# First weights in a free slot, later adaLN pieces, and the norm weight folded into the first tokens of a gated short-convolution layer

## The chip, the core and the metric

The kernel runs on one core of a Trainium2 chip. The metric is the device time of one execution in microseconds. TensorE (PE) does the matrix products, VectorE (DVE) and ScalarE (ACT) the elementwise work, GpSimd (POOL) a few set-up operations, and SyncE (SP) issues nearly all DMA transfers. Each engine works through its own queue in the order in which the program was written down for it, and waits there for semaphores.

## The reference, cut to what matters

One layer is computed in f32, with 256 tokens, D = 2048, E = 4096:

```python
h = rmsnorm(x, norm_g)                       # (256, 2048)
shift, scale, gate = split(silu(c) @ ada_w + ada_b, 3)
h = h * (1.0 + scale) + shift
b_gate, c_gate, v, g = split(h @ w_in, 4)    # w_in (2048, 4 * 4096)
y = b_gate * causal_conv3(c_gate * v, conv_w) * silu(g)
x = x + gate * (y @ w_out)                   # w_out (4096, 2048)
out = rmsnorm(x, final_g)
```

All weights are read once from HBM. f32 products are made of three products of split operands: each weight tile and each activation tile is split into `hi` (rounded to the matmul's format) and `lo` (the remainder), and `hi*hi + hi*lo + lo*hi` is summed.

## The kernel before

**Features.** D is cut into 16 rows of 128, called k. The tokens are scaled by `rstd`, turned by TensorE and kept in `xs[0..3]` (four k in each). When shift and scale of a k are known, `features(k)` writes `hT[:, k]`: ScalarE the rounded half (`hh_`, 128x256), VectorE first the full value back into `xs` and then the remainder (`hl_`).

**adaLN.** Shift and scale come from `ada_w` (2048 rows), for two k at a time: group 0 gives k = 0 and 1, group 1 gives k = 2 and 3, and so on to group 7. Group 0 is loaded whole at the start (`at0`) and summed by VectorE into `gv0`, with three of its 16 rows on TensorE. TensorE then sums over the partitions with `ones` (`sum0(None, ...)`). Every later group is cut into 8 *pieces* of 0.5 MB, each two DMAs and two VectorE operations `gv += at * silu_c`. When a group's last piece is summed, TensorE turns `gv` (`tp_g`, L459, four transposes), ScalarE sums each (L461), VectorE makes shift and scale, and `features` follows for its two k.

**Products of the first half (chunks 0 to 3).** A chunk is 512 columns of one of the four quarters of `w_in`. `plan()` writes out a list of *steps*. A step is one chunk or two, one quarter q, and a stretch of k; per chunk and k there are 12 *products* (L471: 128x128 weights on 128x256 tokens). Steps are numbered from 0 here. Each step takes one *load* of 1 MB per two k (load n belongs to step n up to step 13; load 1 has 0.5 MB), which ScalarE casts into `hi` (*cast n*, L338) and VectorE turns into `lo` (*remainder n*, L339). Loads have three buffers, and so have `hi` and `lo`. Step 0 uses `raw0` (0.5 MB), which takes one of the three load buffers. At a step's end ScalarE copies each chunk's sum from PSUM to SBUF (L503) if it is the chunk's first; a later step of the same chunk either *seeds* PSUM with the kept sum ahead of its products and copies it back behind them (ScalarE, L519 and L503), or adds the kept sum at the end (VectorE, L505). `plan()` decides this by its own estimates of the engines' load.

adaLN pieces are dealt out between loads: every load adds `SHARE` = 1.5 to a `credit`, and each whole unit of it issues one piece. `plan()` also estimates when a group's features are ready, and lets a step's stretch of k reach only that far.

**Around it.** `idle(n, ...)` puts `IDLE[n]` products of ones on TensorE, whose results nobody reads. `pinned` keeps each engine's opening instructions in the order of the code, up to the features of k = 0 and 1; behind that a scheduler places the instructions. After the first half comes the second half of the columns (`mm_b`, from 382 us) and the output products (`mm_o`, from 731 us).

Of the kernel before, what the change touches and what calls it, by code (L numbers as in the profile page):

```python
# [17 lines left out]
KT = D // P  # L18
# [6 lines left out]
CT = 4  # L25
# [29 lines left out]
def plan():  # L55
# [2 lines left out]
    pieces = [(sum(ADA[:g]), nk, i) for g, nk in enumerate(ADA) if g for i in range(4 * nk)]  # L58
    load, pe, dve, act = 0.0, 4.0, 0.0, 0.0
    burst = SLOT // P  # L60
    credit = 0.0

    def ada():
        nonlocal load, dve
# [27 lines left out]
    while new or any(k < KT for k in done.values()):  # L92
        before = []
        hi = sum(r <= pe for r in ready)
        if new:
            p = new.pop(0)
# [32 lines left out]
def short_conv_layer(ctx: ExitStack, tc: tile.TileContext, x, c, norm_g, ada_w, ada_b, w_in, conv_w, w_out, final_g, out):  # L129
    nc = tc.nc  # L130
# [16 lines left out]
    def slot(shape, name, dtype=F32):  # L147
        return slots.tile(shape, dtype, tag="slot", name=name)

    def raw_tile(name):  # L150
        return wpool.tile([P, SLOT], F32, tag="raw", name=name, bufs=3)
# [44 lines left out]
    rows2 = const.tile([96, P], F32, tag="rows2", name="rows2")  # L196
    HX = D // 2
    GIVE = 300
    IDLE = (20, 8, 22, 4, 4, 5, 7, 6)
    xt = [[slot([P, HX], f"x{t}{dh}") for dh in range(2)] for t in range(TT)]  # L200
    for t in range(TT):
        for dh in range(2):
# [8 lines left out]
    for n in range(KT // 4):  # L211
# [5 lines left out]
            for s in range(2):  # L217
                nc.sync.dma_start(at[:, j : j + kk, s, :], adas[:, 4 * n + j : 4 * n + j + kk, s, 0 : NK0 * P])
        first_ada.extend(at[:, i] for i in range(4))
    raw0 = raw_tile("raw0")  # L220
    for k in range(NK0):
        first_load(raw0, k)

# [37 lines left out]
    tp_v = turn(rows1, 0, 64, None)  # L261
    gT = vec[:, 0:16]
    b_shift = vec[:, 16:32]
    b_scale1 = const.tile([P, KT], F32, tag="bsc", name="b_scale1")
    idle(1, turned[2])
    tp_c = turn(rows2, 0, 96, None)
    idle(2, turned[2])
# [43 lines left out]
    def modulate(k0, nk, sums):  # L311

        ks = slice(k0, k0 + nk)
        if nk == 1:
            nc.vector.tensor_scalar(
                out=scale[:, ks], in0=sums[1], scalar1=b_scale1[:, ks], scalar2=gT[:, ks], op0=ALU.add, op1=ALU.mult
            )
            nc.scalar.activation(shift[:, ks], sums[0], AF.Identity, bias=b_shift[:, ks])
        else:
            nc.vector.tensor_tensor(out=scale[:, ks], in0=sums[1], in1=b_scale1[:, ks], op=ALU.add)  # L320
            nc.vector.tensor_tensor(out=scale[:, ks], in0=scale[:, ks], in1=gT[:, ks], op=ALU.mult)
            nc.vector.tensor_tensor(out=shift[:, ks], in0=sums[0], in1=b_shift[:, ks], op=ALU.add)
        for k in range(k0, k0 + nk):
            features(k)

    def features(k):
        hf = xs[k // CT][:, k % CT, :]
        nc.scalar.activation(hh_[:, k], hf, AF.Identity, bias=shift[:, k : k + 1], scale=scale[:, k : k + 1])
        nc.vector.tensor_scalar(
            out=hf, in0=hf, scalar1=scale[:, k : k + 1], scalar2=shift[:, k : k + 1], op0=ALU.mult, op1=ALU.add  # L330
        )
        nc.vector.tensor_tensor(out=hl_[:, k], in0=hf, in1=hh_[:, k].bitcast(F32), op=ALU.subtract)

    def split(raw, n, lo_tag="lo"):
# [25 lines left out]
    for k in range(KT):  # L360
# [2 lines left out]
            nc.vector.tensor_scalar_mul(gv0, first_ada[k], c_k)  # L363
        elif k not in ON_PE:
            nc.vector.scalar_tensor_tensor(out=gv0, in0=first_ada[k], scalar=c_k, in1=gv0, op0=ALU.mult, op1=ALU.add)
    nc.vector.tensor_scalar_add(b_scale1, vec[:, 32:48], 1.0)

    scaled_x(0)
    scaled_x(1)
# [11 lines left out]
    idle(4, turned[3])  # L381
    turn_x(turned[3], 3)
    nc.scalar.copy(xs[3], turned[3])
    tp_idle = psum.tile([P, CT, T], F32, tag="mm", name="tp_idle")
    sum0_of(1)
    idle(5, tp_idle)
# [6 lines left out]
    lo0 = wpool.tile([P, SLOT], F32R, tag="lo", name="lo", bufs=3)  # L393
    w = CT * P
    for k in range(NK0):
        nc.vector.tensor_scalar(
            out=scale[:, k : k + 1], in0=sums0[k][:, 1:2], scalar1=b_scale1[:, k : k + 1], scalar2=gT[:, k : k + 1],
            op0=ALU.add, op1=ALU.mult,
        )
    for k in range(NK0):  # L400
        c = slice(k * w, (k + 1) * w)
        nc.scalar.copy(hi0[:, c], raw0[:, c])
        nc.scalar.activation(shift[:, k : k + 1], sums0[k][:, 0:1], AF.Identity, bias=b_shift[:, k : k + 1])
        nc.vector.tensor_tensor(out=lo0[:, c], in0=raw0[:, c], in1=hi0[:, c].bitcast(F32), op=ALU.subtract)
        features(k)
    pinned.close()
    pieces0 = [(hi0, lo0)]

# [376 lines left out]
```

## Time and profile before

| | |
|---|---|
| median of 3 runs | 915.22 us (914.12 to 916.56) |
| profiled execution | 914.62 us, of which the span from first to last instruction 912.8 us |
| mean granted TensorE clock | 0.996 |
| TensorE busy | 897.6 us, 98% of the span |
| VectorE, ScalarE busy | 628.8 us (69%), 452.3 us (50%) |
| HBM read | 224.49 MB, 248 GB/s over the span |
| first product (L471) | 26.97 us |

Rows of a timeline begin with start and duration in us; a bracket at the end tells how long the engine idled before the row and what ended that. Operands are written output<-input by the tiles' names. A count xN merges equal instructions that follow each other; matmul durations overlap, so starts are to be subtracted, not durations added. A chain is followed back from the last instruction, at each step to what released it; releasers are inferred from semaphore events, and where a wait is for several things it is put down to the one that ended last.

### The profile page before, as it was taken

What the parts mean: (1) busy time and instruction counts of PE and PEld (TensorE: products, weight loads), DVE (VectorE), ACT (ScalarE), POOL (GpSimd) and SP (SyncE); (2) the same over time, 40 slices, a digit from 0 to 9 for tenths busy, and PEclk for the clock granted to TensorE, in tenths of its full rate; (3) what the DMA queues carried; (4) which work ended last, traced back from release to release, by engine and by line L of the source; (5) the groups of instructions that cost most, each with busy time, mean ns of one, the idle gap of its engine ahead of it and who ended that gap; (6) DMA issues with size and microseconds to landing.
All of it is one profiled execution on the core that took longest, in us unless ns stands there. A gap on an engine that the chain in (4) does not pass through costs nothing.

```text
span 912.8 us, 16305 instructions
## 1 busy us (share of the span) xinstructions
PE 897.6 (98%) x7091; PEld 865.4 (95%) x7091; DVE 628.8 (69%) x603; ACT 452.3 (50%) x431; POOL 2.3 (0%) x9
## 2 busy tenths in 40 slices
PE   7899999999999999999999999999999999999996
PEld 7899999999999999999999999999999988888885
DVE  5888989899988998995555455545455544555882
ACT  6678876544545755554333443334433333443333
POOL 1000000000000000000000000000000000000000
PEclk9999999999999999999999999999999999999999
DMA  9999999999898778876655666656656486665542
GB/s 307 377 379 358 339 353 340 353 343 345 295 352 284 254 250 279 284 235 210 201 190 186 191 200 204 190 185 193 199 193 198 142 333 224 201 201 193 185 139 92
DMA packets 146775, 227.64 MB, mean 249 GB/s; under 512 B 5456, under 2 KB 103808, under 8 KB 146320
## 3 DMA queue, kind: packets, MB, share of 16 engines
q1 hardware_dynamic: 146576, 226.51, 73.8%
q8 instruction: 55, 0.90, 0.4%
q14 instruction: 16, 0.13, 0.0%
q0 software_dynamic: 96, 0.08, 0.0%
q10 hardware_dynamic: 32, 0.01, 0.0%
HBM read 224.49 MB, written 2.10 MB: 248 GB/s over the span
## 4 chain that ended last, share of the span: by engine, by line
PE 94%; DMA 3%; ACT 2%; issue 0%; ACTq 0%; SPq 0%; DVE 0%
PE mm_b L471 38%; PE mm_s L471 36%; PE mm_o L681 6%; PE mm_o L682 6%; PE mm_o L683 6%; DMA at<-in_ada_w_dram 3%; ACT hi L338 1%; DMA x<-in_x_dram 1%; ACT mm_s L519 0%; ACT acc L503 0%; PE tp_g L459 0%; PE ps_gate L620 0%; ACT tp_g L461 0%; ACT big L695 0%; ACT big L692 0%
## 5 line engine op out<-in xcount | busy, mean ns | idle before, releaser
L471 PE MATMUL mm_b<-hT,hi 128*128 128x256 f32 x2048 | 348.4, 276 | 0.0
L471 PE MATMUL mm_s<-hT,hi 128*128 128x256 f32 x2048 | 336.6, 277 | 1.5 <-ACT hi L338 1.2
L471 PEld LDWEIGHTS mm_b<-hT,hi 128*128 128x128 f32 x2048 | 308.3, 188 | 0.0
L471 PEld LDWEIGHTS mm_s<-hT,hi 128*128 128x128 f32 x2048 | 299.5, 188 | 2.0 <-ACT hi L338 1.4
L471 PE MATMUL mm_b<-hT,lo 128*128 128x256 f32 x1024 | 282.6, 276 | 0.0
L471 PE MATMUL mm_s<-hT,lo 128*128 128x256 f32 x1024 | 262.2, 277 | 0.0
L339 DVE TENSOR_TENSOR lo<-raw,hi 128x2048 fp32r<-128x2048 f32 x64 | 146.7, 2292 | 130.1 <-ACT hi L338 130.1
L338 ACT CAST hi<-raw 128x2048 fp32r<-128x2048 f32 x64 | 122.5, 1913 | 197.6 <-PE mm_b L471 150.5
L471 PEld LDWEIGHTS mm_b<-hT,lo 128*128 128x128 f32 x1024 | 192.2, 188 | 0.1
L471 PEld LDWEIGHTS mm_s<-hT,lo 128*128 128x128 f32 x1024 | 183.1, 188 | 0.0
L338 ACT CAST hi<-raw_s 128x2048 fp32r<-128x2048 f32 (+1 forms) x64 | 121.7, 1901 | 93.2 <-PE mm_s L471 78.6
L339 DVE TENSOR_TENSOR lo<-raw_s,hi 128x2048 fp32r<-128x2048 f32 (+1 forms) x64 | 145.4, 2271 | 23.9 <-ACT hi L338 23.4
L339 DVE TENSOR_TENSOR lo<-raw_o,hi 128x2048 fp32r<-128x2048 f32 x32 | 73.3, 2290 | 65.2 <-ACT hi L338 65.2
L338 ACT CAST hi<-raw_o 128x2048 fp32r<-128x2048 f32 x32 | 61.0, 1907 | 106.8 <-PE mm_o L683 84.0
L682 PE MATMUL mm_o<-lo,y 128*128 128x512 f32 x256 | 99.3, 389 | 0.0
L683 PE MATMUL mm_o<-hi,y 128*128 128x512 f32 x256 | 99.3, 389 | 0.0
L681 PE MATMUL mm_o<-hi,y 128*128 128x512 f32 x256 | 99.3, 389 | 0.0
L452 DVE SCALAR_TENSOR_TENSOR gv<-at,silu_c,gv 128x512 f32<-128x512 f32 x105 | 78.5, 749 | 2.5 <-DMA at<-in_ada_w_dram 0.9
L683 PEld LDWEIGHTS mm_o<-hi,y 128*128 128x128 f32 x256 | 48.0, 188 | 10.0
L681 PEld LDWEIGHTS mm_o<-hi,y 128*128 128x128 f32 x256 | 48.1, 188 | 10.0
L682 PEld LDWEIGHTS mm_o<-lo,y 128*128 128x128 f32 x256 | 48.0, 188 | 9.9
L503 ACT COPY acc<-mm_s 128x1024 f32<-128x1024 f32 x43 | 43.6, 1018 | 27.9 <-PE mm_s L471 27.8
(107 smaller groups left out, 385.8 us busy)
## 6 DMA issues: line engine op xcount, KB each, us to landing
raw<-in_sc_w_in_dram SPq DMA_DIRECT2D x64, 1024.0 KB, 5.7
raw_s<-in_sc_w_in_dram SPq DMA_DIRECT2D x63, 1024.0 KB, 7.2
raw_o<-in_sc_w_out_dram SPq DMA_DIRECT2D x32, 1024.0 KB, 5.2
at<-in_ada_w_dram SPq DMA_DIRECT2D x126, 256.0 KB, 7.3
at_g<-in_ada_w_dram SPq DMA_DIRECT2D x32, 512.0 KB, 6.6
x<-in_x_dram SPq DMA_DIRECT2D x4, 512.0 KB, 6.6
big<-in_x_dram SPq DMA_DIRECT2D x2, 1024.0 KB, 8.6
out_dram<-big SPq DMA_DIRECT2D x4, 512.0 KB, 2.9
```

The lines of the kernel that those rows point to most:

```text
L338: nc.scalar.copy(hi[:, :n], raw[:, :n])
L339: nc.vector.tensor_tensor(out=lo[:, :n], in0=raw[:, :n], in1=hi[:, :n].bitcast(F32), op=ALU.subtract)
L452: nc.vector.scalar_tensor_tensor(out=gv, in0=at4[:, i], scalar=c_k, in1=gv, op0=ALU.mult, op1=ALU.add)
L471: mm = last_mm[0] = nc.tensor.matmul(dst, w, h[:, k], start=begins and left, stop=ends, skip_group_check=True)
L503: nc.scalar.copy(acc[ch, q], bank)
L681: nc.tensor.matmul(po, yh, hi[:, o], start=opens, stop=False, skip_group_check=True)
L682: nc.tensor.matmul(po, yh, lo[:, o], start=False, stop=False, skip_group_check=True)
L683: nc.tensor.matmul(po, yl, hi[:, o], start=False, stop=ct == NCT - 1, skip_group_check=True)
```

## The change

Four edits. `raw0` is taken from the pool of general slots instead of from the three load buffers. `credit` starts at -1.5, so each piece is issued one load later; since `plan()` also moves its estimates, the list of steps changes. The norm weight is multiplied into `xs[0]` for k = 0 and 1 by ScalarE as soon as that tile is there, so that shift and scale of these k are made by one VectorE operation per k (`sh_sc`), ScalarE's separate `shift` going away. And idle products are moved: `IDLE` 22 to 20 ahead of the transposes, 7 to 11 ahead of group 0's last sums, 6 to 4 behind them; their number stays 76.

```diff
-    credit = 0.0
+    credit = -1.5
...
-    IDLE = (20, 8, 22, 4, 4, 5, 7, 6)
+    IDLE = (20, 8, 20, 4, 4, 5, 11, 4)
...
-    raw0 = raw_tile("raw0")
+    raw0 = slot([P, NK0 * CT * P], "raw0")
...
-    b_scale1 = const.tile([P, KT], F32, tag="bsc", name="b_scale1")
+    b_scale1 = vec[:, 32:48]
+    b_both = vec[:, 16:48].rearrange("p (s k) -> p s k", s=2)
+    sh_sc = const.tile([P, KT // 2, 2], F32, tag="shsc", name="sh_sc")
...
-            features(k)
+            features(k, scale[:, k : k + 1], shift[:, k : k + 1])
...
-    def features(k):
+    def features(k, sc, sh):
...
     nc.scalar.copy(xs[3], turned[3])
+    for k in range(NK0):
+        nc.scalar.activation(xs[0][:, k, :], xs[0][:, k, :], AF.Copy, scale=gT[:, k : k + 1])
...
     for k in range(NK0):
-        nc.vector.tensor_scalar(
-            out=scale[:, k : k + 1], in0=sums0[k][:, 1:2], scalar1=b_scale1[:, k : k + 1], scalar2=gT[:, k : k + 1],
-            op0=ALU.add, op1=ALU.mult,
-        )
+        nc.vector.tensor_tensor(out=sh_sc[:, k], in0=sums0[k][:, 0:2], in1=b_both[:, :, k], op=ALU.add)
     for k in range(NK0):
         c = slice(k * w, (k + 1) * w)
         nc.scalar.copy(hi0[:, c], raw0[:, c])
-        nc.scalar.activation(shift[:, k : k + 1], sums0[k][:, 0:1], AF.Identity, bias=b_shift[:, k : k + 1])
         nc.vector.tensor_tensor(out=lo0[:, c], in0=raw0[:, c], in1=hi0[:, c].bitcast(F32), op=ALU.subtract)
-        features(k)
+        features(k, sh_sc[:, k, 1:2], sh_sc[:, k, 0:1])
```

The list of steps: steps 0 to 7 are the same (k = 0 and 1 of all chunks but the last quarter of chunks 2 and 3). Before, step 8 covers k = 0 to 3 and steps 9 to 11 are the short two-chunk steps over k = 2 and 3 that follow (seeds: both chunks, one, both). Now step 8 covers k = 0 and 1 alone, and steps 9 to 13 are the short ones (both, one, both, one, both). In all there are 32 steps for 30, 34 seeds for 27 and 12 additions by VectorE for 15. Loads stay 65.

SyncE's queue where the first loads end, before: `raw_116` is the first weights' two halves, `raw_s` a load, `at` a piece's DMA.

```order
L188 DMA raw_116<-in_sc_w_in_dram 128x512 x2
L533 DMA raw_s<-in_sc_w_in_dram 128x2x512
L438 DMA at<-in_ada_w_dram 128x2x256 x2
L533 DMA raw_s<-in_sc_w_in_dram 128x2x1024
L438 DMA at<-in_ada_w_dram 128x2x256 x6
L533 DMA raw_s<-in_sc_w_in_dram 128x2x1024 x2
L438 DMA at<-in_ada_w_dram 128x2x256 x4
```

And now:

```order
L188 DMA raw_116<-in_sc_w_in_dram 128x512 x2
L531 DMA raw_s<-in_sc_w_in_dram 128x2x512
L531 DMA raw_s<-in_sc_w_in_dram 128x2x1024
L436 DMA at<-in_ada_w_dram 128x2x256 x2
L531 DMA raw_s<-in_sc_w_in_dram 128x2x1024
L436 DMA at<-in_ada_w_dram 128x2x256 x6
L531 DMA raw_s<-in_sc_w_in_dram 128x2x1024 x2
L436 DMA at<-in_ada_w_dram 128x2x256 x2
```

Load 2 stands ahead of the first piece and load 3 ahead of the second; loads 4 and 5 have the same bytes ahead of them or fewer by two pieces. ScalarE's queue at the first casts, before (the COPY to `acc_364` belongs to step 0, the one to `acc_403` to step 1):

```order
L328 ACTIVATE hT<-xs_212,shift,scale 128x256
L338 CAST hi<-raw_s 128x1024
L503 COPY acc_364<-mm_s 128x1024
L338 CAST hi<-raw_s 128x2048
L503 COPY acc_403<-mm_s 128x1024
```

And now:

```order
L330 ACTIVATE hT<-xs_210,sh_sc 128x256
L338 CAST hi<-raw_s 128x1024
L338 CAST hi<-raw_s 128x2048
L501 COPY acc_364<-mm_s 128x1024
L338 CAST hi<-raw_s 128x2048
L501 COPY acc_397<-mm_s 128x1024
```

Cast 2 has moved ahead of the copy of step 0. VectorE's queue around the end of group 1's sums, before (`lo_480`, `lo_545` and `lo_615` are remainders 3 to 5, `gv_373` is group 1's sum, `at_...` its pieces, `gv_707` opens group 2):

```order
L339 TENSOR_TENSOR lo_480<-raw_s_477,hi_479 128x2048
L452 SCALAR_TENSOR_TENSOR gv_373<-at_548,silu_c_133,gv_373 128x512 x2
L339 TENSOR_TENSOR lo_545<-raw_s_542,hi_544 128x2048
L452 SCALAR_TENSOR_TENSOR gv_373<-at_553,silu_c_133,gv_373 128x512 x2
L452 SCALAR_TENSOR_TENSOR gv_373<-at_618,silu_c_133,gv_373 128x512
L339 TENSOR_TENSOR lo_615<-raw_s_612,hi_614 128x2048
L452 SCALAR_TENSOR_TENSOR gv_373<-at_618,silu_c_133,gv_373 128x512
L452 SCALAR_TENSOR_TENSOR gv_373<-at_683,silu_c_133,gv_373 128x512 x2
L450 TENSOR_SCALAR gv_707<-at_708,silu_c_133 128x512
```

And now (`gv_407` is group 1's sum, `lo_605` to `lo_830` are remainders 5 to 8; remainder 4 stands right ahead of the first row, and ahead of that one four more of the group's sums):

```order
L450 SCALAR_TENSOR_TENSOR gv_407<-at_478,silu_c_133,gv_407 128x512
L339 TENSOR_TENSOR lo_605<-raw_s_602,hi_604 128x2048
L450 SCALAR_TENSOR_TENSOR gv_407<-at_478,silu_c_133,gv_407 128x512
L450 SCALAR_TENSOR_TENSOR gv_407<-at_543,silu_c_133,gv_407 128x512 x2
L339 TENSOR_TENSOR lo_675<-raw_s_672,hi_674 128x2048
L450 SCALAR_TENSOR_TENSOR gv_407<-at_608,silu_c_133,gv_407 128x512 x2
L450 SCALAR_TENSOR_TENSOR gv_407<-at_613,silu_c_133,gv_407 128x512 x2
L339 TENSOR_TENSOR lo_740<-raw_s_737,hi_739 128x2048
L450 SCALAR_TENSOR_TENSOR gv_407<-at_678,silu_c_133,gv_407 128x512 x2
L450 SCALAR_TENSOR_TENSOR gv_407<-at_743,silu_c_133,gv_407 128x512
L339 TENSOR_TENSOR lo_830<-raw_s_827,hi_829 128x2048
L450 SCALAR_TENSOR_TENSOR gv_407<-at_743,silu_c_133,gv_407 128x512
```

Before, group 1's last sum follows remainder 5; now it follows remainder 8. On TensorE group 1's four transposes (`tp_g`) stand behind 240 products before, and behind 298 now. The first product that uses k = 2 is number 385 in both (within step 8 before, the first of step 9 now).

More of the change, by code (lines that the diff above doesn't have):

```diff
@@ L323, in modulate @@
         for k in range(k0, k0 + nk):
-            features(k)
-    def features(k):
+            features(k, scale[:, k : k + 1], shift[:, k : k + 1])
+    def features(k, sc, sh):
         hf = xs[k // CT][:, k % CT, :]
-        nc.scalar.activation(hh_[:, k], hf, AF.Identity, bias=shift[:, k : k + 1], scale=scale[:, k : k + 1])
-        nc.vector.tensor_scalar(
-            out=hf, in0=hf, scalar1=scale[:, k : k + 1], scalar2=shift[:, k : k + 1], op0=ALU.mult, op1=ALU.add
-        )
+        nc.scalar.activation(hh_[:, k], hf, AF.Identity, bias=sh, scale=sc)
+        nc.vector.tensor_scalar(out=hf, in0=hf, scalar1=sc, scalar2=sh, op0=ALU.mult, op1=ALU.add)
         nc.vector.tensor_tensor(out=hl_[:, k], in0=hf, in1=hh_[:, k].bitcast(F32), op=ALU.subtract)
@@ L365, in short_conv_layer @@
             nc.vector.scalar_tensor_tensor(out=gv0, in0=first_ada[k], scalar=c_k, in1=gv0, op0=ALU.mult, op1=ALU.add)
-    nc.vector.tensor_scalar_add(b_scale1, vec[:, 32:48], 1.0)
+    nc.vector.tensor_scalar_add(b_scale1, b_scale1, 1.0)
     scaled_x(0)
@@ L395, in short_conv_layer @@
     for k in range(NK0):
-        nc.vector.tensor_scalar(
-            out=scale[:, k : k + 1], in0=sums0[k][:, 1:2], scalar1=b_scale1[:, k : k + 1], scalar2=gT[:, k : k + 1],
-            op0=ALU.add, op1=ALU.mult,
-        )
+        nc.vector.tensor_tensor(out=sh_sc[:, k], in0=sums0[k][:, 0:2], in1=b_both[:, :, k], op=ALU.add)
     for k in range(NK0):
```

## The prediction

> **What bounds the kernel now.** I read the page first, then TensorE's waits, then the chain in order of time, then each engine's timeline up to 130 us. In the page's first part and its fourth, the chain that ended last:
>
> ```profile
> PE 897.6 (98%) x7091; PEld 865.4 (95%) x7091; DVE 628.8 (69%) x603; ACT 452.3 (50%) x431; POOL 2.3 (0%) x9
> ...
> PE 94%; DMA 3%; ACT 2%; issue 0%; ACTq 0%; SPq 0%; DVE 0%
> ```
>
> TensorE carries the span: no edit removes a product, so time can come only from where TensorE stands still or runs slowly. Its waits (total, times, longest) that touch the change:
>
> ```profile
> PE sum L351 <- DVE gv L365: 1.2, 1, 1.2
> PE mm_s L471 <- ACT hi L338: 1.2, 1, 1.2
> ...
> PE mm_s L471 <- ACT mm_s L519: 0.3, 1, 0.3
> ```
>
> Next TensorE's timeline at the opening (start, duration, instruction, count, idle before it), and three rows of the chain, which merge its stretches:
>
> ```profile
> 24.37 1.31 PE L351 MATMUL sum<-ones,gv 128*128 128x1 f32 x8 [1.22 <-DVE gv L365]
> 25.54 1.63 PE L254 MATMUL tp_idle<-ones_r 128*128 128x256 f32 x6
> 26.97 1.05 PE L471 MATMUL mm_s<-hT,hi 128*128 128x256 f32 x4
> ...
> 34.47 3.90 PE L471 MATMUL mm_s<-hT,hi 128*128 128x256 f32 x32 [1.20 <-ACT hi L338]
> ...
> 34.47 22.03 PE mm_s L471 x192
> 56.51 0.44 PE tp_g L459 x4
> 56.94 24.51 PE mm_s L471 x216
> ```
>
> Products start at 26.97, the first 48 (steps 0 and 1) are done at 34.47 - 1.20 = 33.27, step 2 starts at 34.47, and group 1 is turned (tp_g) behind product 240. A product takes 24.51 / 216 = 0.1135 us. Why step 2 is late stands in ScalarE's timeline:
>
> ```profile
> 24.14 0.62 ACT L402 CAST hi<-raw 128x512 fp32r<-128x512 f32 x1 [2.71 <-DMA raw<-in_sc_w_in_dram]
> 25.39 0.26 ACT L403 ACTIVATE shift<-sum,vec 128x1 f32<-128x1 f32 x1 [0.63 <-DVE scale L396]
> 25.68 0.60 ACT L328 ACTIVATE hT<-xs,shift,scale 128x256 fp32r<-128x256 f32 x1
> ...
> 31.61 1.02 ACT L503 COPY acc<-mm_s 128x1024 f32<-128x1024 f32 x1 [3.09 <-PE mm_s L471]
> 32.52 1.90 ACT L338 CAST hi<-raw_s 128x2048 fp32r<-128x2048 f32 x1
> 34.32 1.02 ACT L503 COPY acc<-mm_s 128x1024 f32<-128x1024 f32 x1
> 37.29 1.92 ACT L338 CAST hi<-raw_s 128x2048 fp32r<-128x2048 f32 x1 [1.95 <-DMA raw_s<-in_sc_w_in_dram]
> ```
>
> Cast 2 (at 32.52) stands behind the copy of step 0, which waited 3.09 us for TensorE. Its own data were there: loads land in issue order, and a piece issued after load 2 was consumed at 31.86 (below). The chain ascribes that time to an adaLN transfer, which ended at the same moment.
>
> VectorE's timeline is what the forecast rests on:
>
> ```profile
> 25.02 0.28 DVE L396 TENSOR_SCALAR scale<-sum,b_scale,vec 128x1 f32<-128x1 f32 x1 [0.62 <-PE sum L351]
> ...
> 31.86 1.54 DVE L452 SCALAR_TENSOR_TENSOR gv<-at,silu_c,gv 128x512 f32<-128x512 f32 x2 [0.90 <-DMA at<-in_ada_w_dram]
> 34.45 2.29 DVE L339 TENSOR_TENSOR lo<-raw_s,hi 128x2048 fp32r<-128x2048 f32 x1 [1.05 <-ACT hi L338]
> 36.66 3.11 DVE L452 SCALAR_TENSOR_TENSOR gv<-at,silu_c,gv 128x512 f32<-128x512 f32 x4
> 39.69 2.29 DVE L339 TENSOR_TENSOR lo<-raw_s,hi 128x2048 fp32r<-128x2048 f32 x1
> ...
> 50.74 2.32 DVE L452 SCALAR_TENSOR_TENSOR gv<-at,silu_c,gv 128x512 f32<-128x512 f32 x3
> 52.98 0.48 DVE L450 TENSOR_SCALAR gv<-at,silu_c 128x512 f32<-128x512 f32 x1
> ```
>
> From start to start a remainder takes 36.66 - 34.45 = 2.21 us, four sums 39.69 - 36.66 = 3.03, three 52.98 - 50.74 = 2.24. Group 1's last sum ends near 53.0; TensorE asks for it at 56.51, so there are 3.5 us to spare.
>
> **The opening, part by part.** The norm weight: two activations on 128x256 join ScalarE between its last xs copy and 24.14, in the 2.71 us it sat idle for the first weights; between 0.26 and 0.60 us each by the rows above, so nothing. Two shift activations (0.26 each) leave, and one tensor_tensor per k takes the place of the scale (0.28): the first feature is ready at 25.02 + 0.28 + 0.60 = 25.95 instead of 26.28. TensorE does not ask for it then: six idle products run until 26.97, at (26.97 - 25.54) / 6 = 0.24 us each. Two fewer give 0.48: products start at 26.49. Four more idle products ahead of the last sums fit into the 1.22 us wait (0.11 each at the full clock); whether they hold the clock up is open:
>
> ```profile
> 21.57:24.99 3.42, 2.21 (x19) 2.00 (x19) 2.02 (x4) 0.62 (x1) 0.00 (x0) 1.00 1.05 360
> 24.99:28.40 3.41, 3.41 (x17) 3.41 (x18) 2.89 (x8) 2.95 (x6) 0.00 (x0) 0.50 1.02 378
> 28.40:31.81 3.41, 3.41 (x32) 3.41 (x31) 2.57 (x4) 0.32 (x2) 0.00 (x0) 1.00 1.08 355
> ```
>
> (busy time of PE, PEld, DVE, ACT, POOL in the stretch, then granted clock, DMA share, GB/s). The clock was halved for 3.41 us right behind the stretch with the 1.22 us wait. If it stays up, idle products and first products cost half and the start is about 25.9, held by the first feature. So step 2 is reached at 33.27 - 0.48 = 32.8 (halved) or 25.95 + 48 x 0.1135 + 0.2 for remainders = 31.6 (full).
>
> Load order and slot: load 2 now goes ahead of piece 0 (0.5 MB) and cast 2 ahead of the copy of step 0. It landed by 31.86 less one piece; a piece takes 0.52 MB / 0.374 MB per us = 1.4 us at this rate:
>
> ```profile
> 20.00:40.00 20.00, 17.58 (x137) 17.18 (x137) 15.30 (x24) 11.44 (x14) 0.00 (x0) 0.91 1.05 374
> ```
>
> so it lands near 31.86 - 1.4 - 1.4 = 29.1 and cast 2 ends at 31.0, before TensorE wants it. The 1.20 us wait goes. Step 2 is 1.7 to 2.9 us earlier. That is the gain on offer.
>
> **Where most of it is given back: group 1.** The DMA share is above 1.00 there: the stream is full, so the order of loads decides, and a buffer that comes free sooner (the slot) brings no more bytes. Load 4 has the same bytes ahead of it as before (loads 1 to 3, four pieces), and load 3, issued just before it, landed at 37.29: load 4 lands at 37.29 + 1.05 / 0.374 = 40.1. Cast 4 ends at 42.0. In VectorE's queue remainder 4 stands ahead of 12 of group 1's 16 operations and, with the pieces a load later, loads 7 and 8 now come before the last one too. From 42.0 VectorE has five remainders, 5 x 2.21 = 11.05, and twelve sums in runs of 1, 3, 4, 3, 1, that is 0.70 + 2.24 + 3.03 + 2.24 + 0.75 = 8.96: the last ends at 62.0. TensorE's turn now stands behind product 298, reached at step 2's start + 250 x 0.1135 = 28.4, so 60.0 to 61.2. It waits 0.8 to 2.0 us whichever clock it had, and goes on at 62.0 + 0.44 = 62.45. Before, it was past product 298 at 56.94 + 58 x 0.1135 = 63.52. **Gain left: 1.07.**
>
> Then the features of k = 2 and 3, which product 385 is the first to need. ScalarE and VectorE at those of before:
>
> ```profile
> 59.54 0.26 ACT L461 ACTIVATE tp_g<-tp_g 128x128 f32<-128x128 f32 x1
> ...
> 59.95 0.26 ACT L461 ACTIVATE tp_g<-tp_g 128x128 f32<-128x128 f32 x1
> ...
> 60.73 1.02 ACT L503 COPY acc<-mm_s 128x1024 f32<-128x1024 f32 x1
> ...
> 64.36 1.10 ACT L328 ACTIVATE hT<-xs,shift,scale 128x256 fp32r<-128x256 f32 x2
> ...
> 66.46 0.73 DVE L329 TENSOR_SCALAR xs<-xs,scale,shift 128x256 f32<-128x256 f32 x2
> 67.11 0.74 DVE L452 SCALAR_TENSOR_TENSOR gv<-at,silu_c,gv 128x512 f32<-128x512 f32 x1
> 67.77 0.75 DVE L332 TENSOR_TENSOR hT<-xs,hT 128x256 fp32r<-128x256 f32 x2
> ```
>
> Cast 10 needs the buffer that step 7 frees at product 336: 62.45 + 38 x 0.1135 = 66.8, end 68.7; remainder 10 until 70.95, the scalings 0.65, a sum 0.66, the first hl 0.4: 72.65. TensorE has done 384 products at 62.45 + 86 x 0.1135 = 72.2. It waits 0.45. **Gain left: 0.62.**
>
> Last, ScalarE in the short steps. Two-chunk steps over two k last 48 x 0.1135 = 5.45 us, and a seeded chunk costs ScalarE two copies (from start to start 32.52 - 31.61, some 0.92 each); a group costs four sums at 0.41 and two features, 2.6:
>
> ```profile
> 80.00:100.00 20.00, 19.69 (x173) 19.49 (x172) 18.29 (x23) 19.76 (x27) 0.00 (x0) 1.00 0.99 331
> ```
>
> Before there are three of them, with 3 casts, 5 seeds and a group: 5.7 + 9.2 + 2.6 = 17.5 in 16.35 us, for which TensorE paid 0.31. Now there are five, with 5 casts and 8 seeds: 9.5 + 14.7 + 2.6 = 26.8 in 27.2. Full, not overfull: waits between 0 and the 1.9 us of one cast. Adding up ScalarE's queue from 72.65 on (the copy out of a finished chunk, the next seed, a cast when a step frees its buffer), the seeds of step 10 (first chunk), 11 (second) and 13 (first) come some 0.1, 0.2 and 0.4 late; I take 0.5 in all, 0.2 more than before. The seven more seeds in all (34 for 27) and three fewer additions (12 for 15) fall in stages where both engines have time.
>
> **Sum:** -1.07 + 0.45 + 0.2 = -0.4 us. The profiled execution took 914.62 (span 912.8 and 1.8 around it) and would take 914.2; the median of the runs is 0.6 above it, so **914.8**.
>
> **The rivals.** (1) The opening's gain stays, because VectorE reaches group 1's last sum before TensorE asks. For it: the 3.5 us to spare before. Against: it needs the sum by 60.0 to 61.2. Gain 1.7 to 2.9 plus some of the 0.31, about 2.4: 912.8. (2) The short steps cost more, as ScalarE at 19.76 of 20 says it can; each further missed seed is 1 us, so about 1.5 more: 916.3. (3) Slower than before: the new stall of TensorE at product 298 halves its clock for a stretch, as the 1.22 us one at the opening did; that costs 3.41 / 2 = 1.7 a time, so 916.5, and beyond 0.3% with two stretches, 918.2. It decides if the stall comes near 2 us and few products lie about it; against it, the 1.20 us wait at 33.27 left the clock at 1.00. The Trainium skill (TensorE: Matmul & The Clock Gate, Part 1) has the clock halved after at least one idle window of about 3.4 us; by that rule a 2 us stall costs nothing more and the time stays 914.8. The drop after only 1.22 us of idling speaks against taking the rule as it stands. (4) The slot and the later pieces change nothing because cast 2 is still late: 915.2.
>
> **How the numbers follow.** Forecast 0.55, (1) 0.17, (2) 0.15, (3) 0.08, (4) 0.05. Within 0.3% (2.7 us, about what a measurement of this kernel can tell from no change; its three runs spread over 2.4) lie the forecast, (2), (4), most of (3), and the half of (1) that is under 2.7: 0.87. Faster 0.09: the rest of (1). Slower 0.04: two slow stretches. The range goes from rival (1) to a little beyond (2) and (3), 912.7 to 916.9.
>
> **What would show it.** Right: products start by 26.5, no wait at step 2, a TensorE wait of 0.8 to 2.0 at tp_g for VectorE's gv near 62, small waits near 72 for hT or mm_s. Wrong: no wait at tp_g (rival 1); many waits for L517 or hT before 100 us (2); granted clock 0.50 near 62 (3). The forecast fails if load 4 lands elsewhere than 40, since each us of it moves the tp_g wait by one.

## The result and the profile after

The changed kernel took 920.1 us (median of 6 runs, 918.5 to 923.6), the kernel before 915.2 beside it: ratio 1.0058, interval 1.0036 to 1.0079. It is slower by 0.6%, and outside the range of 912.7 to 916.9. The profiled execution took 923.62 (span 921.8), 3.5 above its median, so a second profile of the same kernel (a_again) is used beside it. The first part of the page, and TensorE's waits behind the first product:

```profile
PE 901.1 (98%) x7091; PEld 867.5 (94%) x7091; DVE 626.7 (68%) x600; ACT 467.0 (51%) x445; POOL 2.3 (0%) x9
```

```profile
PE mm_s L469 <- ACT acc L501: 3.1, 1, 3.1
PE mm_s L469 <- DVE acc L503: 2.4, 1, 2.4
...
PE mm_s L469 <- ACT mm_s L517: 0.9, 2, 0.5
PE mm_s L469 <- DVE lo L339: 0.8, 2, 0.5
PE sum L351 <- DVE gv L365: 0.4, 1, 0.4
```

The wait for a cast (`hi` L338) at step 2 is gone; a wait for a copy out of PSUM (`acc` L501), which no step of the prediction has, is the largest. TensorE's timeline shows where:

```profile
25.23 1.20 PE L254 MATMUL tp_idle<-ones_r 128*128 128x256 f32 x4
26.23 1.05 PE L469 MATMUL mm_s<-hT,hi 128*128 128x256 f32 x4
...
32.81 3.00 PE L469 MATMUL mm_s<-hT,hi 128*128 128x256 f32 x25
...
40.07 1.07 PE L469 MATMUL mm_s<-hT,lo 128*128 128x256 f32 x8
44.20 2.61 PE L469 MATMUL mm_s<-hT,hi 128*128 128x256 f32 x16 [3.06 <-ACT acc L501]
```

The opening is as forecast: first product at 26.23, step 2 at 32.81 without a wait, 1.66 us earlier than before. Then TensorE stops for 3.06 us behind product 120, in the middle of step 3. ScalarE's timeline at that place:

```profile
33.81 1.91 ACT L338 CAST hi<-raw_s 128x2048 fp32r<-128x2048 f32 x1 [1.29 <-DMA raw_s<-in_sc_w_in_dram]
35.63 1.01 ACT L501 COPY acc<-mm_s 128x1024 f32<-128x1024 f32 x1
41.34 1.90 ACT L338 CAST hi<-raw_s 128x2048 fp32r<-128x2048 f32 x1 [4.70 <-DMA raw_s<-in_sc_w_in_dram]
43.14 1.01 ACT L501 COPY acc<-mm_s 128x1024 f32<-128x1024 f32 x1
44.05 1.91 ACT L338 CAST hi<-raw_s 128x2048 fp32r<-128x2048 f32 x1
```

The row at 41.34 is cast 4, which stands 4.70 us waiting for load 4. Behind it in the queue stands the copy of step 2's first chunk (43.14), whose products were done at 32.81 + 24 x 0.1135 = 35.5. In the kernel before both copies of step 2 stood ahead of cast 4:

```profile
39.31 1.94 ACT L503 COPY acc<-mm_s 128x1024 f32<-128x1024 f32 x2
41.13 1.92 ACT L338 CAST hi<-raw_s 128x2048 fp32r<-128x2048 f32 x1
```

Three PSUM banks (`mm`) go round over the chunks, so step 3's second chunk needs the bank of step 2's first: it starts when the copy ends. The chain of waits names load 4, cast 4 and this copy in a row:

```profile
31.19 10.07 DMA raw_s<-in_sc_w_in_dram
41.34 1.90 ACT hi L338
43.23 0.92 ACT acc L501
44.20 22.11 PE mm_s L469 x178
```

The clock pays for it too. Busy time in three stretches (PE, PEld, DVE, ACT, POOL), then granted clock, DMA share, GB/s:

```profile
40.00:45.70 5.70, 2.64 (x23) 2.44 (x22) 2.43 (x2) 4.36 (x3) 0.00 (x0) 1.00 1.04 384
45.70:49.10 3.40, 3.40 (x18) 3.40 (x17) 3.39 (x3) 3.21 (x4) 0.00 (x0) 0.50 0.92 292
49.10:52.50 3.40, 3.40 (x32) 3.40 (x31) 3.34 (x3) 2.58 (x3) 0.00 (x0) 1.00 1.02 389
```

18 products instead of 32 in 3.40 us. A second loss lies late in the first half of the columns. VectorE's timeline (`gacc` are the sums of adaLN's gate, `at_g` their loads of 0.5 MB, issued at L602), then TensorE's:

```profile
330.16 0.48 DVE L609 TENSOR_SCALAR gacc<-at_g,silu_c 128x512 f32<-128x512 f32 x1
330.68 0.75 DVE L611 SCALAR_TENSOR_TENSOR gacc<-at_g,silu_c,gacc 128x512 f32<-128x512 f32 x1
331.42 2.29 DVE L339 TENSOR_TENSOR lo<-raw_s,hi 128x2048 fp32r<-128x2048 f32 x1
339.35 0.75 DVE L611 SCALAR_TENSOR_TENSOR gacc<-at_g,silu_c,gacc 128x512 f32<-128x512 f32 x1 [5.64 <-DMA at_g<-in_ada_w_dram]
340.02 2.28 DVE L339 TENSOR_TENSOR lo<-raw_s,hi 128x2048 fp32r<-128x2048 f32 x1
```

```profile
357.64 0.50 PE L469 MATMUL mm_s<-hT,hi 128*128 128x256 f32 x2 [2.43 <-DVE acc L503]
363.83 0.51 PE L469 MATMUL mm_s<-hT,hi 128*128 128x256 f32 x2 [0.47 <-ACT mm_s L517]
```

VectorE stands 5.64 us at a gate sum, with remainders and additions queued behind it, and TensorE runs out of them some 16 us later. In the whole program such waits at L611 came to 13.8 us (total, times, longest), with 0.6 more at L609, and before to 1.9 at the two lines of these sums:

```profile
DVE gacc L611 <- DMA at_g<-in_ada_w_dram: 13.8, 5, 5.6
```

Counting TensorE's products in order gives where time went. The table has the start of a product less its start before (negative is earlier), from one profile each; product 49 opens step 2, 121 is step 3's second chunk, 577 lies behind the short steps, 2841 near the end of the first half.

| kernel | 49 | 121 | 145 | 289 | 577 | 2401 | 2841 |
|---|---|---|---|---|---|---|---|
| changed | -1.66 | +1.46 | +2.86 | +2.78 | +3.64 | +3.62 | +8.92 |
| a_again (same kernel) | -1.77 | +2.23 | +3.97 | +3.52 | +4.37 | +4.39 | +6.10 |
| a_cast4 | -2.17 | -2.15 | -2.10 | -0.26 | +0.58 | +0.56 | +2.88 |
| a_own | -2.90 | -0.07 | +1.23 | +1.83 | +2.73 | +2.76 | +1.79 |
| a4_own | -3.66 | -3.77 | -3.76 | -1.53 | -0.62 | -0.62 | -1.59 |
| b_own | -1.17 | -0.64 | -0.64 | -0.64 | -0.63 | -0.70 | -1.67 |

So the two profiles of the changed kernel have a first loss of 3.1 to 4.0 us at product 121 with 1.4 to 1.7 more up to 145, and a late loss of 1.7 to 5.3 between 2401 and 2841. From 2841 on nothing changes. (Kernels with "own" have four of the gate's eight products, `ps_gate`, moved behind 2841: 0.97 us that comes back by product 5001.) One thing varies from execution to execution in this table: the clock was halved in the opening in the first two rows and in the kernel before, and not in the other four rows, which is worth up to 1.7 us at product 49 (see the last section).

### The profile page after: what moved, and what is told of

Same layout as the page of the kernel before. It is cut to its first block, busy times and chain, and to the rows that moved or that the text cites. A ratio compares the mean times of both kernels' runs of the same rounds, so it can differ in the third digit from the quotient of the medians.

```text
span 921.8 us, 16333 instructions
## 1 busy us (share of the span) xinstructions
PE 901.1 (98%) x7091; PEld 867.5 (94%) x7091; DVE 626.7 (68%) x600; ACT 467.0 (51%) x445; POOL 2.3 (0%) x9
## 4 chain that ended last, share of the span: by engine, by line
PE 83%; DMA 7%; DVE 5%; ACT 2%; issue 1%; SPq 0%; ACTq 0%; DVEq 0%
PE mm_b L469 38%; PE mm_s L469 26%; PE mm_o L681 6%; PE mm_o L680 6%; PE mm_o L679 6%; DMA at_g<-in_ada_w_dram 3%; DMA at<-in_ada_w_dram 2%; DVE lo L339 2%; DMA raw_s<-in_sc_w_in_dram 1%; DVE gacc L611 1%; ACT hi L338 1%; DMA x<-in_x_dram 1%; ACT mm_s L517 0%; ACT acc L501 0%; DVE acc L413 0%
## 5 line engine op out<-in xcount | busy, mean ns | idle before, releaser
L469 PE MATMUL mm_s<-hT,hi 128*128 128x256 f32 x2048 | 340.4, 278 | 6.4 <-ACT acc L501 3.1
L469 PE MATMUL mm_s<-hT,lo 128*128 128x256 f32 x1024 | 266.2, 278 | 0.9 <-DVE lo L339 0.8
L338 ACT CAST hi<-raw 128x2048 fp32r<-128x2048 f32 x64 | 122.5, 1913 | 202.1 <-PE mm_b L469 150.8
L469 PEld LDWEIGHTS mm_s<-hT,lo 128*128 128x128 f32 x1024 | 185.2, 189 | 1.5 <-DVE lo L339 1.5
L338 ACT CAST hi<-raw_s 128x2048 fp32r<-128x2048 f32 (+1 forms) x64 | 121.4, 1898 | 83.2 <-PE mm_s L469 69.2
L338 ACT CAST hi<-raw_o 128x2048 fp32r<-128x2048 f32 x32 | 61.0, 1907 | 106.8 <-PE mm_o L681 84.0
L501 ACT COPY acc<-mm_s 128x1024 f32<-128x1024 f32 x50 | 50.3, 1013 | 12.4 <-PE mm_s L469 12.4
```

The costliest lines, as they stand in the source:

```text
L338: nc.scalar.copy(hi[:, :n], raw[:, :n])
L469: mm = last_mm[0] = nc.tensor.matmul(dst, w, h[:, k], start=begins and left, stop=ends, skip_group_check=True)
L501: nc.scalar.copy(acc[ch, q], bank)
```

## The experiments

The theory of the first loss, A: cast 4, ahead of the copies of step 2 and waiting for load 4, keeps a PSUM bank from TensorE. The theories of the late loss: late loads through SyncE's in-order queue, or the gate's sums at that place of VectorE's queue at all. The other letters are explained in the expectations that use them. Ratios are to the kernel before on the same chip.

**a_again: the changed kernel once more.**

> The changed kernel once more, to have its profile from another execution and its time on the same chip as the next three. Both theories: about 920 us, 4.9 above before, with a wait of TensorE near 41 us (behind product 120) and waits between 310 and 365 us. If the clock was halved behind the first wait only by chance, this profile shows less than the 3.6 us that the first one had lost by product 577.

919.3 us, ratio 1.0050 (1.0036 to 1.0064). The wait behind product 120 was 3.95 us, the halved stretch 45.5 to 48.9; the late loss 1.7. The first loss is steady, the late one varies.

**a_cast4: cast 4 alone behind the two copies of step 2.**

```diff
-            nc.scalar.copy(acc[ch, q], bank)
+            cp = nc.scalar.copy(acc[ch, q], bank)
+            kept.setdefault(n_step[0], []).append({cp.ins.engine: cp.ins.name})
...
-            with behind(ended if first_pieces else {}):
+            with behind(ended if first_pieces else {}), behind(kept[2][1] if n_step[0] == 4 else {}):
```

> Changed kernel with one cast moved: cast 4 stands behind both copies of step 2 in ScalarE's queue. a_casts moved five casts and the scheduler moved much else with them; this one moves less. Theory A (the PSUM bank of step 3's second chunk is freed by a copy that stands behind cast 4, which waits for load 4): no wait behind product 120, product 145 some 1.5 to 1.9 us earlier than in before instead of 2.9 to 4.0 later. Theory E (a second lock stands behind the first: features of k = 2 and 3 come late because adaLN's pieces are a load later): the lead is gone by product 385, and products 385 to 577 lose more, with waits for hT, for seeds and a halved clock; total 917 to 925. Rival (the cast was all of it): the lead of 1.5 stays at product 577 and the total is 915.5 to 917, what the late stage (310 to 365 us) costs.

(`kept[n]` holds the copies of step n, `n_step[0]` counts the steps, and `behind` places an instruction behind another of its engine.) 916.2 us, ratio 1.0020 (1.0011 to 1.0028). ScalarE's rows: the copies go at 36.27, ahead of the cast.

```profile
36.27 2.83 ACT L501 COPY acc<-mm_s 128x1024 f32<-128x1024 f32 x3
41.39 1.92 ACT L338 CAST hi<-raw_s 128x2048 fp32r<-128x2048 f32 x1 [2.29 <-DMA raw_s<-in_sc_w_in_dram]
...
48.09 1.92 ACT L338 CAST hi<-raw_s 128x2048 fp32r<-128x2048 f32 x1 [1.29 <-DMA raw_s<-in_sc_w_in_dram]
49.91 2.83 ACT L501 COPY acc<-mm_s 128x1024 f32<-128x1024 f32 x3
```

The wait behind 120 and the halved stretch are gone, and the median is 3.1 to 3.9 us lower: A holds. The lead that TensorE had there is gone all the same by product 385 (+0.19), and the late loss stays (2.3 in this profile). The same thing happens again on a small scale at cast 6 (48.09, waiting for its load ahead of three copies), and TensorE waits 1.02 behind product 192.

**a_casts: casts 4 to 8 each behind both copies of the step two before** (the same edit with `4 <= n_step[0] <= 8`).

> Changed kernel, with casts 4 to 8 of ScalarE's queue put behind the copies of the step two before (cast 4 behind both copies of step 2). Theory A (cast 4 stands in ScalarE's queue ahead of the copy that frees the PSUM bank of step 3's second chunk, and waits there for its DMA): the 3.06 us wait goes, and with it the half clock behind it (1.7), so 3.1 to 4.8 us less than the changed kernel, 915.3 to 917. Rival B (load 4 itself is late): TensorE only waits a little further on, at step 4, and the time stays at 920. If the forecast of VectorE's queue holds, a wait at tp_g for gv of 2 to 4 us takes its place, and the gain is 1 to 2 us only.

927.9 us, ratio 1.0150 (1.0130 to 1.0169): a miss. The wait behind 120 went (product 145 at -3.71), but the scheduler placed everything behind it anew, and three waits behind products 384 to 386 halved the clock for two stretches in a row (product 577 at +6.33). The late loss was 7.0 us here, with one more halved stretch at 362.01:

```profile
51.84 1.21 PE L469 MATMUL mm_s<-hT,lo 128*128 128x256 f32 x8 [1.89 <-DVE lo L339]
...
73.78 0.38 PE L469 MATMUL mm_s<-hT,hi 128*128 128x256 f32 x1 [0.98 <-ACT hT L330]
76.08 0.58 PE L469 MATMUL mm_s<-hT,hi 128*128 128x256 f32 x1 [1.92 <-ACT mm_s L521]
77.03 1.24 PE L469 MATMUL mm_s<-hT,hi 128*128 128x256 f32 x2 [0.36 <-ACT mm_s L521]
```

**a_credit0, a_noslot, b_cd, b_slot: parts of the change.** a_credit0 is the changed kernel with `credit = 0.0`; a_noslot has `raw0 = raw_tile("raw0")` again; b_cd has both of these, which leaves the norm weight and the idle products; b_slot is the kernel before with only the slot.

> Changed kernel with the credit back at 0.0, so the list of steps and the pieces of before; slot, norm weight and idle products stay changed. In ScalarE's queue cast 4 still stands ahead of the copy of step 2's first chunk. Theory F (the slot makes the early cast, the credit makes the late stage): a wait of 2.5 to 4 us behind product 120 stays, the waits past 310 us go, total 917 to 918.5. Rival (the credit makes both): no wait behind 120, total 913.5 to 914.5.

> Changed kernel with raw0 back in the three load buffers; credit, norm weight and idle products stay changed. In ScalarE's queue cast 4 stands behind the copies of step 2 again, and pieces are issued in fours. Theory F: no wait behind product 120, but the late stage loses 1.7 to 5.3 us, total 916 to 919. Rival (the slot makes both): no loss in either place, 914 to 915.

> Kernel before with the norm weight in the first tokens and the idle products of the change, without slot and credit. All theories: products start 0.5 to 1.0 us earlier; cast 2 stands behind the copy of step 0 as in before, which moves with the start, so step 2 comes 0.5 to 1.0 earlier and nothing else changes: 914.2 to 914.7. If idle products or the new feature code cost something by themselves, it is over 915.2.

> The kernel before, with only the first weights in a free slot. Theory O (whatever brings the casts earlier lets the scheduler put cast 4 ahead of copies of step 2, as its order on ScalarE shows here too; the loss goes with that order, not with the clock's lead or the norm weight): a wait behind product 120 for a bank of 1 to 4 us, 916 to 919 us. Rival (the slot alone gives its 1.2 us wait at step 2 back and costs nothing): 914 to 915 us.

| | us | ratio (interval) | largest waits of TensorE behind the first product |
|---|---|---|---|
| a_credit0 | 916.4 | 1.0017 (1.0009 to 1.0026) | 0.93 at product 48 (`hi`), 1.06 at 120 (`acc` L501) |
| a_noslot | 918.0 | 1.0026 (1.0016 to 1.0037) | 2.99 at 96 (`hi`: cast 3) |
| b_cd | 918.2 | 1.0040 (1.0028 to 1.0052) | 1.20 at 48, 1.96 at 96 (`hi`), 1.04 at 626 (a seed) |
| b_slot | 917.0 | 1.0026 (1.0017 to 1.0034) | 1.11 at 120 (`acc` L503), 1.06 at 387 (`hT`) |

Each costs 1.4 to 3.1 us (medians, against 915.06 beside them; 915.11 for b_slot), and no profile of them shows the late loss. With the slot, the copy that frees a bank is late. Without it, load 3 stands behind four pieces (a_noslot, b_cd) and lands no earlier than before (37.6 and 37.2, before 37.2), while product 49 starts 3.4 and 1.6 us earlier: TensorE waits for cast 3, and the stretch behind that wait is at half clock in both. So the expectations of a_credit0 (2.5 to 4 us behind product 120; 1.06 measured), a_noslot (the late loss stays) and b_cd (914.2 to 914.7) failed, and the slot and the credit are not each the cause of one loss. By these profiles the late loss needs slot and credit together, that is one particular order of the whole program, not the list of steps, which a_noslot has too. There is one profile of each, and a_noslot's runs go from 914.9 to 919.5 with the profiled one at 916.3, so where its slower runs lose the rest is open.

**a_gates, a_both: the gate's loads behind the last load of the first half** (a_both with the casts of a_casts).

```diff
+        with behind(last_load):
             nc.sync.dma_start(at3, adas[:, j : j + 2, 2, dc * 512 : (dc + 1) * 512])
```

> Changed kernel, with the DMAs of the gate pieces (at_g) put behind the last load of the first half in SyncE's queue, so that their sums fall into the second half. Theory C (VectorE stands in its queue in front of gate sums whose DMAs are behind loads, and the loads behind VectorE's remainders): the waits between 310 and 365 us go, 3.7 to 5.3 us less than the changed kernel, 914.8 to 916.4. Rival D (the new list of steps gives VectorE more to do there whatever the gates do): some of those waits stay, 918 or more.

> Changed kernel with both edits. Theories A and C: the two gains add up, and the opening's 1.7 us (product 49 at 32.8 instead of 34.5) comes through as far as VectorE's queue lets it: 913.5 if group 1 is no bound, 914.6 if TensorE waits at tp_g as the prediction walked it. Rivals B and D: 918 or more.

924.2 us, ratio 1.0106 (1.0087 to 1.0124), and 929.4, ratio 1.0164 (1.0143 to 1.0185). Both are misses. The late loss was gone in a_gates (product 2401 at +3.67, 2841 at +2.70), but 54 of the gate's 64 sums now came in the second half, where TensorE waited for remainders and lost 9.9 us up to the end (0.97 of it the moved gate products):

```profile
PE mm_b L470 <- DVE lo L339: 6.3, 7, 1.4
```

**a_gpool, a4_gpool: the gate's loads from GpSimd's queue** (`nc.gpsimd.dma_start`; a4_gpool with a_cast4's edit).

> The changed kernel with the gate's loads (at_g, L602) issued by GpSimd's queue instead of SyncE's; the order of everything on TensorE, VectorE, ScalarE up to there is as in the changed kernel. Theory Q (the late loss, 310 to 365 us, is the in-order queue of SyncE: a gate load stands there behind first-half loads that wait 4 to 11 us for VectorE's remainders, and VectorE then stands at the gate's sum): the wait of VectorE at L611 for at_g (5.6 us in the stretch) goes, and product 2841 starts about as late as product 577 (+3.6 to +4.4) instead of +6.1 to +8.9; the first stall, behind product 120, stays; 917 to 918 us. Rival D (the transfers themselves share the bandwidth, or VectorE's sums and remainders are too much work there): product 2841 still +6 to +9, 919 to 920 us.

> As a_gpool, and cast 4 behind the copies of step 2 (as in a_cast4, 916.2 us). If both losses are as theory A (a PSUM bank's copy behind a cast that waits for load 4) and theory Q (SyncE's queue) say and they are independent: a_cast4's late +2.3 goes, end at +0.3 to +0.8 against before, 913.5 to 914.7 us. Rival D: as a_cast4, 916.2. Rival: GpSimd's earlier gate loads collide with the loads of the steps and something else waits: 917 or more.

920.9 us, ratio 1.0066 (1.0052 to 1.0080), and 919.0, ratio 1.0040 (1.0027 to 1.0053); the late loss was 6.4 and 5.2 us in their profiles. That the loads stand behind others in SyncE's queue is not the cause. GpSimd's timeline and VectorE's of a_gpool:

```profile
321.69 0.72 POOL L602 DMA_DIRECT2D at_g<-in_ada_w_dram  x1 [18.84 <-DVE gacc L611]
330.59 0.72 POOL L602 DMA_DIRECT2D at_g<-in_ada_w_dram  x1 [8.18 <-DVE gacc L611]
342.51 0.72 POOL L602 DMA_DIRECT2D at_g<-in_ada_w_dram  x1 [11.20 <-DVE gacc L611]
```

```profile
329.54 0.75 DVE L611 SCALAR_TENSOR_TENSOR gacc<-at_g,silu_c,gacc 128x512 f32<-128x512 f32 x1
330.27 2.29 DVE L339 TENSOR_TENSOR lo<-raw_s,hi 128x2048 fp32r<-128x2048 f32 x1
338.59 0.75 DVE L611 SCALAR_TENSOR_TENSOR gacc<-at_g,silu_c,gacc 128x512 f32<-128x512 f32 x1 [6.03 <-DMA at_g<-in_ada_w_dram]
```

In a queue of its own a load still goes out only when VectorE's sum of the piece before has ended (329.54 + 0.75 = 330.29, issue at 330.59), takes 8 us, and is wanted one remainder later. So at this place the loads go out one by one, though the pool has four buffers.

**a_own, a4_own, b_own: the gate's split sums (`gate_s`) in a slot** instead of one of those four buffers; a4_own with a_cast4's edit, b_own on the kernel before. Slots come free late, so the sums of the third and fourth quarter of the gate move behind the first half (32 of 64 stay in it, 63 in the changed kernel).

```diff
-            parts = adap.tile([P, 2, 512], F32R, tag="at", name="gate_s", bufs=4)
+            parts = slot([P, 2, 512], "gate_s", F32R)
```

> The changed kernel with the gate's split sums (gate_s) in a slot instead of in one of the four buffers of the pieces. The first 200 us are issued as in the changed kernel; slots come free late, so the gate's third and fourth quarter (and their loads and sums) move behind the first half of the program, away from 310 to 365 us. Theory B (gate sums in VectorE's queue, each waiting for a load that could start only when the sum before had freed a buffer, hold up the remainders there): no wait of VectorE at L611 between 310 and 365, product 2841 as late as product 577 (+3.6 to +4.4), the first stall stays: 917.5 to 919 us unless the moved sums make waits in the second half. Rival W (the short seeded steps are too much work for ScalarE and VectorE there by themselves): product 2841 still +6 or more. Rival M (the moved sums cost as much in the second half, as in a_gates): waits for VectorE's remainders after 400 us, 920 or more.

> As a_own, and cast 4 behind the copies of step 2 (a_cast4: 916.2 us, +0.56 at product 577, +2.9 at the end). Theory B: no late loss, product 2841 at +0.2 to +0.8, 913.9 to 914.9 us. Rival W: +2.9 stays, 916.2. Rival M: waits after 400 us, 917 or more.

> The kernel before with gate_s in a slot alone. It had no wait of TensorE between 310 and 390 us, so the moved gate sums have nothing to give there: 914.3 to 915.2 us, ratio 0.9995 to 1.0005. Rival (the moved sums are a gain by themselves and a4_own owes its time to that): 913.5 or less.

916.7 us, ratio 1.0021 (1.0012 to 1.0030); **914.1, ratio 0.9996 (0.9987 to 1.0004)**; and 914.2, ratio 0.9986 (0.9977 to 0.9995). The stretch of the late loss in the changed kernel and in a_own (columns as above; PE first):

```profile
310.00:365.00 55.00, 51.17 (x436) 49.87 (x435) 49.32 (x58) 36.52 (x38) 0.00 (x0) 1.00 0.64 223
```

```profile
310.00:365.00 55.00, 55.00 (x487) 55.00 (x487) 46.84 (x55) 38.60 (x40) 0.00 (x0) 1.00 0.57 192
```

The seeded steps with their seeds are still there, the gate's sums are not, and TensorE has no wait. The sums alone do no harm: between products 2401 and 2841 the kernel before has 12 of them, more than the changed kernel with 10, and VectorE waits for none of their loads. What costs time is an order in which each stands ahead of remainders while its load is still under way. Two small edits take both losses away, 5.2 to 6.0 us, and leave no measurable difference to the kernel before. b_own has the lowest ratio, 0.14% under the kernel before, so nothing shows that the change is a gain over that edit alone. The gain of b_own was not expected. Its profile has no wait removed, but the clock stayed at 1.00 through the opening, where the profile before has 0.50 for 3.41 us, and from product 121 on its lead is the same 0.6 to 0.7 us (but for the moved gate products). Whether its other runs gain in that way is open.

**a0_cast4, aF48_own, a0F48_own, aF46_own: other orders of the casts.** a0_cast4 is a_cast4 with credit 0.0. In the F kernels a cast stands behind the copy of the first chunk of the step two before: casts 4 to 8 (F48, a0F48 with credit 0.0) or 4 and 6 (F46), all with `gate_s` in a slot.

> The changed kernel with credit 0.0 (adaLN's pieces as before the change), and cast 4 behind the copies of step 2. a_credit0 had 916.4 with a wait of 1.06 for a bank behind product 120 and no late loss. Theory A: that wait goes, product 121 before -1.0, and what is left of it after group 1 is little, since VectorE's chain and the later casts then set the time (a_cast4 kept none of its -2.1 by product 385): 914.8 to 916.2 us. Rival (lead is kept, since without the credit the pieces come earlier): 913 to 914 us.

> As a_own, with casts 4 to 8 each behind the copy of the first chunk of the step two before, which is the copy that frees the bank for the step's second chunk (rule from the first loss; it also takes away a_cast4's wait of 1.0 us at product 192). If the banks' copies alone cost the lead: product 289 at -1 to -1.5, then group 1 and the later casts cost 0.6 to 1.5, end -0.5 to +0.5, 913.5 to 914.8 us. Rival: as a_casts, where casts 4 to 8 behind both copies moved the seeds and gave 5 to 6 us of waits at products 384 to 387 and a halved clock: 918 or more.

> As aF48_own with credit 0.0, so adaLN's pieces by the old list of steps. a0_cast4 was 915.1 with waits of 1.29 (product 48), 0.64, 0.75 and 0.55 and ended at +1.5. Without the waits for banks (0.75) and with the gate's sums moved: 914 to 915 us. Rival (load 3 behind the pieces and VectorE's chain take the same time again): 915 to 916.5.

> As a4_own, with casts 4 and 6 (not 5, 7, 8) behind the copy of the first chunk of the step two before, so that the wait of 1.0 us at product 192 goes too. If waits for banks set the time there: product 289 at -2.5, end at about -1.6, 913.0 to 913.9 us: a version faster than both. Rival (the loads set the time between 40 and 60 us, the DMA share is 1.02 to 1.10 there in every kernel): the wait turns into one for a remainder or a cast, product 289 at -1.0 to -1.8 as in a4_own, 913.9 to 915.

915.1 us (ratio 1.0001, 0.9991 to 1.0010), 916.6 (1.0024, 1.0014 to 1.0033), 918.6 (1.0039, 1.0025 to 1.0052) and 917.0 (1.0016, 1.0008 to 1.0025). In a0_cast4 the wait behind product 120 (1.06 in a_credit0) is gone too and the median is 1.3 us lower (916.4 without its edit), as A has it; its profile, 1.2 above its median, doesn't show the gain, since other waits took as much by product 577 (+1.71, a_credit0 +1.83). The F kernels missed: with casts 5 to 8 moved, seeds and features behind products 384 to 387 come late (1.73 and 1.44 in aF48_own, 1.81 in a0F48_own) and the clock is halved. aF46_own moved the wait of 1.0 us from product 192 to 144; in its profile the clock was halved for 6.83 us in the opening, and product 49 came 3.8 us later than in a4_own, which is more than the difference at the end. No order tried has a lead of more than 0.62 us (a4_own) at product 577; aF48_own had 2.68 at product 289 and lost it to the late seeds and features.

## Why the prediction was wrong, step by step

**The opening** was right in mechanism and size: start 26.23 for 26.49, step 2 at 32.81 for 32.8, its wait of 1.20 gone, the clock halved as in the first of the two cases. The second case came in other executions: in a_own's profile the clock stayed at 1.00, with products from 25.77 (forecast 25.9) and step 2 at 31.57 (31.6). What decides between them, left open there, is in the last section. (The first feature's sum, 25.02 + 0.28 + 0.60, is 25.90, not 25.95; nothing hangs on it.)

**The step that failed** is the walk from step 2 to group 1, which has TensorE run through 250 products without a wait. It worked out that load 4 lands at 40.1 (measured: 41.26) and charged that to VectorE, in whose queue remainder 4 stands ahead of the sums. It didn't ask what stands behind cast 4 in ScalarE's queue: the copy that frees the bank for step 3's second chunk. TensorE needed the bank at 41.14, some 20 us before the wait forecast for group 1. That is 3.06 to 3.95 us and a halved stretch of 1.4 to 1.7, and without it (a_cast4) 3.1 to 3.9 us of the 4.9 are back. The later landing is not what failed: in a_own load 4 landed at 39.73, and TensorE waited 2.78 us all the same.

**Group 1.** The walk along VectorE's queue held: the group's last sum ended at 62.57 in a_own (forecast 62.0) and, with load 4 later, at 63.76 in the changed kernel. But TensorE, held up before, came to the turn only at 66.15:

```profile
63.02 0.74 DVE L450 SCALAR_TENSOR_TENSOR gv<-at,silu_c,gv 128x512 f32<-128x512 f32 x1
66.15 0.60 PE L457 MATMUL tp_g<-ident,gv 128*128 128x128 f32 x4
```

The wait of 0.8 to 2.0 us at the turn came in none of the profiles, with the first loss or without it. In a_cast4, where the turn came at 63.45, the lead of 2.10 at product 145 was gone behind it (+0.19 at 385; forecast behind the turn -1.07). Most of it went in short waits ahead of the turn, for remainder 4 at 45.69 and for a bank at 50.97. By the starts of the products around them, which include the slow first product behind a wait, they cost 0.45 and 1.29 us:

```profile
45.69 1.21 PE L469 MATMUL mm_s<-hT,lo 128*128 128x256 f32 x8 [0.18 <-DVE lo L339]
50.97 2.10 PE L469 MATMUL mm_s<-hT,hi 128*128 128x256 f32 x16 [1.02 <-ACT acc L501]
```

The forecast of 0.45 at product 385 for `hl` was wrong: no kernel that kept the list of steps waited there unless casts beyond 4 and 6 were moved.

**The short steps** cost one wait of 0.43 to 0.45 behind product 576 for a seed, where 0.5 in three places was forecast (0.31 before). It was so in nine of the thirteen profiles with that list of steps; the other four, with other orders of the casts or without the slot, had no such wait there.

**"Fall in stages where both engines have time"** was wrong for the late stage, a second term put at nothing: the new order put the gate's sums where each waits for its load, 1.7 to 5.3 us.

**The rivals.** Of the mechanisms listed, (3), the halved clock behind a stall, happened, at another stall. A stall that the walk doesn't contain was in none of them, so the chance of 0.04 for slower stood for too little. With both losses taken out (a4_own) the time is 914.1, near the forecast of 914.8, but that nearness is luck: the lead left behind the turn (-1.02 at product 385 in its profile, forecast -1.07) came of an opening at full clock and of waits for a remainder and a bank, not of a wait for group 1.

## What to carry to other kernels

When a change moves an instruction ahead in an in-order queue, ask of each instruction now behind it what it frees and who needs that (here a PSUM bank), and price the case that the moved one's data are late. Time won ahead of a stage is kept only if what the stage waits for comes earlier too: load 4 landed at 39.91 before and at 39.65 in a4_own, whose lead of 3.76 us at product 145 was 0.62 at product 577. Where a scheduler places the instructions, compare the order of the whole program: here four kernels with only parts of the change each lost 1.4 to 3.1 us, by waits at places that the parts don't name. And before two profiles are compared, see whether the opening's clock was the same in both.

## What the runs showed of the hardware

The clock's rule came out sharper than expected. Halved stretches are 3.41 us long or twice that, and within one execution they lie on a fixed grid (a_casts: 75.29 and 362.01, 84.0 times 3.413 apart). Over the 20 profiles, cutting each timeline into that grid from 30 us on and adding up TensorE's idle time in each piece gives: the next piece was halved in all 12 cases with 1.82 to 2.99 us idle (at full clock until then), and in none of the 27 with 0.93 to 1.72. So about half a piece of idling decides, and where the stall falls on the grid: 3.17 us in a_gpool were cut into 1.72 and 1.45 and cost nothing more, 1.82 in a_casts, all in one piece, halved the clock.

The opening fits the same border if the time under products of one column (`sum`, 128x1) is counted as idle. Between 14 and 34 us, pieces with 1.75 to 2.34 us so counted were followed by a halved one in all 7 cases, and those with up to 1.56 in none. In the changed kernel's profile the wait for `gv` was down to 0.41 us, but with the `sum` products it comes to 1.86. The grid lies otherwise in each execution, so the same opening is halved in one and not in the next: before has 2.34 in one piece, b_own, whose opening is the same, 1.50 and 1.56 in two. Over the runs of the kernel before that stand beside the experiments, those with a mean clock of 0.995 took 916.5 us (median of 22) and those with 0.998 took 913.7 (14).

The Trainium skill (TensorE: Matmul & The Clock Gate, Part 1) describes a free-running window of 3413 ns, which these runs agree with. It has the clock halved after at least one idle window, which is more than was needed here, since half a window was enough.
